# Loads of x, of its copy by tokens, of residuals and of factor sources tied behind the weights' loads in issue order, in an attention and pooling trunk

## The chip, the cores and the metric

The kernel runs on one core of a Trainium2 chip. Its time is the device time of one execution in microseconds (us), taken as the median of several runs. All transfers of this kernel are issued by one engine's queue, SyncE's (SP in the profile), and are carried by the core's 16 DMA engines.

## The reference

The program is a trunk of two layers over 4,096 tokens of width 1,024, all in float32, with a norm ahead of each layer, a residual after it and a norm at the end.

```python
for i in range(DEPTH):                       # DEPTH = 2
    h = rmsnorm(x, norm_g[i])
    y = attn_layer(h, ...) if i % 2 == 0 else pool_layer(h, ...)
    x = x + y
return rmsnorm(x, final_g)
```

The attention layer makes q (16 heads of 64), k and v (4 heads each) and a gate z with one projection, attends in a sliding window of 128 tokens with a learned sink per head, multiplies by silu(z) and projects back. The pool layer makes u and z, takes trailing means of u over 2, 4, 8 and 16 tokens, mixes them, gates and projects back.

## The kernel before

A float32 operand is split into a high and a low part, and each product is three passes of TensorE (`PASSES`, line 261). The attention layer goes over 8 groups of 512 tokens, called stages here, s = 0 to 7. A stage has up to 14 units of 48 matmuls of 128x512 each: `k`, `q0` to `q3`, `v`, `out0` to `out3` (the output projection of the group before) and `z0` to `z3`. A stage of s from 2 to 6 runs k, q0, v, out0, out1, q1, out2, q2, out3, z0, q3, z1, z2, z3; the units are numbered through, so that stage 2 has units 24 to 37, with v as unit 26, and the v units of stages 3 to 7 are 40, 54, 68, 82 and 96. The v unit is written the other way round, as 96 matmuls of 128x256 (line 280): `v_piece` goes over the four blocks of 128 tokens, and for each block first over the first four chunks of the width and then over the last four.

Between the matmuls of the units stand the 16 attention iterations of a stage, each in three steps: scores (`it_scores`, matmuls at line 385, then softmax on VectorE, ScalarE and GpSimd), the turn of the probabilities (`it_turn`, transposes at line 410, a cast at 417, differences at 418 and 425, selections on GpSimd) and the product with v (`it_pv`, matmuls at lines 440 and 441, additions at 448). Names such as `P1_3_2` or `m1_1_3_2` give stage, head group and block.

What moves through SP's queue, in the order of the queue:

- **Weights.** From the second stage on, a unit's split weights come back from memory in two halves of 1 MB (`w_again`, lines 159 to 162; `w26_0` and `w26_1` are the halves of unit 26). They rotate through three buffers, so a half can only be loaded when the half three places before it has been used up: `w26_1` takes the buffer of `w25_0`, which is free when q0 is halfway through.
- **x, transposed** (`xt_load`, line 177): four loads of 512 KB a stage, `xt3_0` to `xt3_3` for stage 3. They are scaled on VectorE by the norm's factors (`x_scale`, line 253) and split into h (`h_chunk`).
- **A copy of x by tokens** (`xm_load`, line 182): four loads of 512 KB that share the two buffers `xt` with the loads before. ScalarE squares and sums each (`xm_square`, line 189).
- **The norm's factors** (`spread`, lines 230 to 246): from the sums, VectorE (`ms`) and GpSimd (`rs`) make 1/root; SP writes it out (`rsq`, line 241) and, once that has landed, reads it back broadcast over the partitions (`bc`, line 245). `x_scale` waits for `bc`.
- **k's second copy** (`k_twice`, line 307): four small transfers `kt<-kt` that follow the casts of k on ScalarE (line 300) and the differences on VectorE (line 301).
- **Residuals** (`res_load`, line 458), 512 KB each, for the four `out` units, and the stores of their results.
- **Factor sources and factors for the pool layer** (`seven_load`, line 515, 512 KB; `seven`, lines 518 to 541): raw weights are loaded, split into parts on ScalarE, VectorE and GpSimd, and stored again (`w_u<-part_u` and the like, lines 524 and 541; in the lists of order `w7_...<-part7_...`).

The order of the work is made in two steps. Each piece is entered with a planned time, in units, by `at(t, fn, ...)`, and the pieces are sorted by it. All of the attention layer is then emitted inside a block with a scheduler (line 1103), which simulates the engines' time and reorders each engine's queue as it sees fit. A load that waits for nothing but a buffer may so be moved ahead of pieces that were planned earlier. The loads of the copy for the next stage were planned at unit 5.0 and after (`XM`, line 39), but stand in the queue at the start of the stage. The pool layer after the attention layer is emitted in the planned order.

Of the kernel before, what the change touches and what calls it, by code (L numbers as in the profile page):

```python
# [1 line left out]

# [33 lines left out]


STRIP = 56
XM = (4.0, 6.3)
SLOTS = dict(sr=1, sl=2)  # L40


# [5 lines left out]
def f32(ap):  # L48
    return ap.bitcast(F32)
# [3 lines left out]
def trunk_kernel(ctx, tc, xt, xm, ng, w_a_in, sinks, w_a_out, wu_t, wmix, pscale, w_b_z, w_b_out, fg, out):  # L53
    nc = tc.nc
# [21 lines left out]
    wparts = {}  # L76
# [62 lines left out]
    def at(t, fn, *args):  # L139
        events.append((t, len(events), fn, args))  # L140


    wtiles = {}
    wraws = {}

    def w_load(U, src, hf):
# [11 lines left out]

    def w_again(U, hf, key):
        t = lp.tile([128, 2, 4, UC], F32R, tag="w", bufs=3, name=f"w{U}_{hf}")  # L160
        nc.sync.dma_start(f32(t), wparts[key, hf])
        wtiles[U, hf] = t


# [5 lines left out]
    def xt_load(s, n):  # L170
        if s > 0:
            t = sp.tile([128, 2, G], F32, tag="xt", bufs=2, name=f"xt{s}_{n}")
        else:
            if n % 2 == 0:
                xts["pair"] = lp.tile([128, 2, 2, G], F32, tag=f"a{2 + n // 2}", name=f"xt{s}_{n}")
            t = xts["pair"][:, n % 2]
        nc.sync.dma_start(t, xt[s, n])
        xts[s, n] = t

    def xm_load(s, b):  # L180
        t = sp.tile([128, D], F32, tag="xt", bufs=2, name=f"xm{s}_{b}")
        nc.sync.dma_start(t, xm[s, b])
        xts[s, "m", b] = t

    def xm_square(s, b):
# [269 lines left out]

    def res_load(s, n):
        t = lp.tile([128, 2, G], F32, tag="res", bufs=2, name=f"res{s}_{n}")
        nc.sync.dma_start(t, xt[s, n])
        ress[s, n] = t

    def ev_o(U, s, n):
# [47 lines left out]
    def seven_load(key, src, hf):  # L509
        if hf == 0 and key[0] == "o":  # L510
            wout[key[1]] = [dram.tile([128, 2, 2, UC], F32, name=f"wo_{key[1]}_{i}") for i in range(4)]
        elif hf == 0:
            wseven[key] = [dram.tile([128, 2, 2, 2, 128], F32, name=f"w7_{key[0]}{key[1]}_{i}") for i in range(7)]
        t = lp.tile([128, 4, UC], F32, tag="wraw", bufs=2, name=f"raw7_{key[0]}{key[1]}_{hf}")
        nc.sync.dma_start(t, src[:, 4 * hf:4 * hf + 4, :])
        wraws[key, hf] = t

    def seven(key, hf):
# [324 lines left out]
    def unit(kind, s, j, t):  # L843
# [8 lines left out]
        if u == 0:  # L852
            for hf in range(2):
                at(-8.85, w_load, u, src, hf)
                at(-8.05, w_split, u, hf, key, nc.gpsimd if hf else nc.vector)
        elif s == 0:
            at(t - T["wl0"], w_load, u, src, 0)
            at(t - T["wl1"], w_load, u, src, 1)
            at(t - T["ws0"], w_split, u, 0, key, nc.gpsimd if kind in "qz" else None)
            at(t - T["ws1"], w_split, u, 1, key, None if kind == "out" else nc.gpsimd)  # L860
        else:
            at(t - T["wr0"], w_again, u, 0, key)
            at(t - T["wr1"], w_again, u, 1, key)
        if kind == "out":
            at(t - T["res"], res_load, s, j)
# [22 lines left out]
    for n in range(4):  # L888
        at(-9, xt_load, 0, n)
# [17 lines left out]
    for s in range(NG + 1):  # L907
# [16 lines left out]
        if s < NG:  # L924
# [7 lines left out]
            for i in range(16):  # L932
                j, b, t = i // 4, i % 4, base + sc[i]
# [3 lines left out]
            for j in range(4):  # L937
                t = max(base + order.index(("z", j)) + 1.0, base + sc[4 * j + 3] + turn + pv)
                at(t, gate_a, s, j)
        if s + 1 < NG:  # L940
            for n in range(4):
                at(base + XM[s > 0] + 0.9 * n - 1.3, xm_load, s + 1, n)
                at(base + XM[s > 0] + 0.9 * n, xm_square, s + 1, n)
                at(base + L + (-3.2, -3.0, -0.74, -0.49)[n], xt_load, s + 1, n)
            at(base + XM[s > 0] + 3.2, spread, s + 1)
            for k in range(NK):
                t = base + L - 1 + (k + 1) / 8 + T["hc"]
                t = base + L + 0.2 if k > 5 else t
                at(t if k > 3 else base + L - T["xs"] + k / 8, x_scale, s + 1, k)
                at(t, h_chunk, s + 1, k)  # L950
        if 2 <= s < NG:
            for i in range(4):
                k, hf = sevens[4 * (s - 2) + i]
                t = base + 2.0 + 3.2 * i
                at(t, seven_load, k, sources[k[0]][k[1]], hf)
                at(t + 0.8, seven, k, hf)
# [27 lines left out]
    for g in range(NP):  # L984
        ph = (g, "in")
        stream = [(ph, kind, j) for j in PAIRS for kind in "uz"]
        if g == 0:
            t0 = base - A_OUT
            at(t0 + 2.0, b_spread, ("h", 0))
            for i, p in enumerate(PAIRS):  # L990
                t = t0 + 6.0 * i
# [52 lines left out]
        for p in PAIRS:  # L1044
            for n in (0, 1):
                t = pos - (0, PROD, 5 * PROD, 7 * PROD)[p] + (0.1 if p > 1 else 0.3 if p else 0.5 + 5 * n)
# [3 lines left out]
        for x, j in enumerate(PAIRS):  # L1050
            u = (po, "o", j)
            at(op - 3.0 if x == 0 else pos - 8.0, o_open, u)
            if g == NP - 1 and x == 3:
                t = pos
# [99 lines left out]
```

## Time and profile before

| what | value |
|---|---|
| runs | 2660.74, 2655.14, 2654.10 us; median 2655.14 us |
| the profiled execution, its own time | 2661.88 us |
| its span, first to last instruction | 2660.1 us |
| TensorE (PE) busy | 2549.5 us, 96% of the span |
| VectorE (DVE), ScalarE (ACT), GpSimd (POOL) busy | 61%, 39%, 22% |
| mean granted TensorE clock | 0.983 of full speed |
| moved by DMA | 626 MB, SP's queue busy 69.7% of 16 engines' span |

The attention layer's stages 2 to 7 lie between 408 and 1613 us. In the profile PE is TensorE's matmul, PEld its weight load, SPq the issue of transfers from SP's queue. "idle before, releaser" is the time for which an engine did nothing ahead of an instruction, and what ended that. In rows of windows, each engine has its busy time with the number of its instructions, and the row ends with the granted clock of TensorE (1.00 is full speed), the mean busy share of the 16 DMA engines, and GB/s.

### The profile page before, as it was taken

Reading aid. Unit: us, or ns where it says so; the run is one execution under the profiler, and the core shown is the slowest. Engines: PE = TensorE matmul, PEld = TensorE weight load, DVE = VectorE, ACT = ScalarE, POOL = GpSimd, SP = SyncE. Lnnn points to the kernel's source line nnn. Section 1 sums busy time; section 2 is a strip of 40 time slices with the busy share of each in tenths; the row PEclk is TensorE's granted clock in tenths of the full one; section 3 lists DMA queues with packets and bytes.
Section 4 is the critical chain, followed back from the end, with each engine's and each line's share of the span. In section 5 each row is a group of like instructions: output and inputs, shape, how many; then the busy total and the mean of one; then the engine's idle time right before and its main releaser. Section 6 shows DMA issues by size and latency. Waiting matters only on the chain.

```text
span 2660.1 us, 35166 instructions
## 1 busy us (share of the span) xinstructions
PE 2549.5 (96%) x12604; PEld 2146.2 (81%) x12604; DVE 1612.3 (61%) x2537; ACT 1043.2 (39%) x2680; POOL 578.7 (22%) x883
## 2 busy tenths in 40 slices
PE   7999999999999999999998999999999999999997
PEld 5888888887887887887887887888878887887886
DVE  5377666566567567566566568648455665655544
ACT  4465545355345445444444443223312231332121
POOL 3554333233243242233332331000000000000000
PEclk8999999999999999999999999999999999999998
DMA  8865766677678677677677657667577668757752
GB/s 289 313 210 192 270 228 230 223 244 256 224 251 277 223 241 250 225 245 257 222 246 239 204 201 273 207 194 260 194 261 265 233 219 289 267 175 262 252 202 99
DMA packets 175193, 626.07 MB, mean 235 GB/s; under 512 B 23198, under 2 KB 33438, under 8 KB 145324
## 3 DMA queue, kind: packets, MB, share of 16 engines
q1 hardware_dynamic: 175020, 623.83, 69.7%
q8 instruction: 100, 1.64, 0.2%
q14 instruction: 73, 0.60, 0.1%
HBM read 489.47 MB, written 117.51 MB: 228 GB/s over the span
## 4 chain that ended last, share of the span: by engine, by line
PE 56%; DMA 16%; DVE 9%; ACT 2%; issue 2%; SPq 0%; POOL 0%; DVEq 0%; POOLq 0%; ACTq 0%
PE mm L270 19%; DMA fin<-x 3%; PE mm L280 3%; DMA w<-wparts 3%; DMA w_u<-part_u 2%; DMA out<-fin 2%; PE s L385 2%; DMA w_z<-part_z 2%; PE X_0u L628 2%; PE X_0z L628 2%; PE X_3z L628 1%; PE X_3u L628 1%; PE po L440 1%; PE X_2u L628 1%; PE pT L410 1%
## 5 line engine op out<-in xcount | busy, mean ns | idle before, releaser
L270 PE MATMUL mm<-h,w 128*128 128x512 f32 x3456 | 848.8, 396 | 9.1 <-DVE sz L354 4.5
L270 PEld LDWEIGHTS mm<-h,w 128*128 128x128 f32 x3456 | 638.5, 190 | 136.8 <-DVE sz L354 5.1
L270 PE MATMUL mm<-a,w 128*128 128x512 f32 x1536 | 372.2, 393 | 4.2 <-DMA w<-wparts 2.5
L270 PEld LDWEIGHTS mm<-a,w 128*128 128x128 f32 x1536 | 282.0, 188 | 61.2 <-issue 2.0
L426 POOL TENSOR_SCALAR_AFFINE_SELECT m<-m 64x256 fp32r<-64x256 f32 x256 | 117.7, 460 | 580.7 <-ACT m L417 572.3
L397 ACT ACTIVATE P<-s,mx 128x129 f32<-128x129 f32 x512 | 181.8, 370 | 34.8 <-DVE mx L394 32.4
L447 ACT COPY tmp<-po 64x256 f32<-64x256 f32 x256 | 94.1, 367 | 198.7 <-PE po L441 164.5
L755 POOL TENSOR_TENSOR rs<-ms,mhalf 128x4 f32<-128x4 f32 x7 | 7.0, 1007 | 735.8 <-DVE ms L754 735.8
L402 POOL TENSOR_TENSOR P<-P,sm 128x516 f32<-128x516 f32 x128 | 138.9, 1085 | 115.3 <-DVE sm L401 114.7
L448 DVE TENSOR_TENSOR o<-po,tmp 64x256 f32<-64x256 f32 x256 | 107.7, 421 | 84.0 <-ACT tmp L447 79.8
L385 PEld LDWEIGHTS s<-kt,q 128*128 128x128 f32 x1024 | 135.0, 193 | 8.7 <-ACT s L376 0.3
L427 POOL TENSOR_SCALAR_AFFINE_SELECT m<-m 64x256 fp32r<-64x256 f32 x256 | 120.2, 470 | 90.2 <-DVE m L425 81.5
L385 PE MATMUL s<-kt,q 128*128 128x192 f32 x1024 | 136.9, 273 | 0.0
L318 DVE SCALAR_TENSOR_TENSOR q<-mm,q 64x512 fp32r<-64x512 f32 x128 | 88.1, 688 | 77.4 <-ACT q L317 75.9
L280 PE MATMUL mm<-w,h 128*128 128x256 f32 x768 | 107.7, 302 | 25.1 <-DMA w<-wparts 25.1
L280 PEld LDWEIGHTS mm<-w,h 128*128 128x128 f32 x768 | 104.5, 210 | 26.9 <-DMA w<-wparts 26.4
L317 ACT ACTIVATE q<-mm 64x512 fp32r<-64x512 f32 x128 | 75.9, 593 | 104.3 <-DVE q L318 58.3
L425 DVE TENSOR_TENSOR m<-pT,m 64x256 fp32r<-64x256 f32 x256 | 108.1, 422 | 7.9
L397 ACT ACTIVATION_READ_ACCUMULATOR P<-s,mx 128x1 f32 x512 | 104.6, 204 | 0.0
L417 ACT CAST m<-pT 128x512 fp32r<-128x512 f32 x128 | 75.0, 586 | 70.7 <-PE pT L410 65.4
L390 DVE COPY_PREDICATED s<-mask,s 128x256 f32<-128x256 int8 x128 | 54.3, 424 | 78.8 <-PE s L385 59.4
L418 DVE TENSOR_TENSOR m<-pT,m 128x512 fp32r<-128x512 f32 x128 | 87.9, 687 | 14.6 <-ACT m L417 12.7
(359 smaller groups left out, 4478.9 us busy)
## 6 DMA issues: line engine op xcount, KB each, us to landing
w<-wparts SPq DMA_DIRECT2D x196, 1024.0 KB
wparts<-w SPq DMA_DIRECT2D x28, 1024.0 KB
xt<-in_xt SPq DMA_DIRECT2D x32, 512.0 KB
res<-in_xt SPq DMA_DIRECT2D x32, 512.0 KB
x<-res SPq DMA_DIRECT2D x32, 512.0 KB
xr<-x SPq DMA_DIRECT2D x32, 512.0 KB
xm<-in_xm SPq DMA_DIRECT2D x28, 512.0 KB
w_u<-part_u SPq DMA_DIRECT2D x56, 256.0 KB
```

The source lines that it names most:

```text
L270: nc.tensor.matmul(ps[:, c], w[:, wl, k % 4, 128 * c:128 * c + 128], rhs(k, hl), start=(k == 0 and i == 0), stop=(k == NK - 1 and i == 2))
L280: nc.tensor.matmul(ps[:, b], hts[s, k][:, hl, 128 * b:128 * b + 128], wtiles[U, k // 4][:, wl, k % 4], start=(k == 0 and i == 0), stop=(k ...
L318: nc.vector.scalar_tensor_tensor(dst[64 - r:128 - r], src, -SCALE, f32(dst[r:r + 64]), op0=ALU.mult, op1=ALU.subtract)
L385: nc.tensor.matmul(ps[:, 2 * c + u, 2 - 2 * u:194 - 2 * u], qs[s, j][:, c, 2 * b + u].rearrange("p r x -> p (r x)"), kt[:, j, hl, t:t + 19 ...
L397: nc.scalar.activation(P[:, i, 0:129], view(ps, 1 + 512 * (i // 2) + 319 * (i % 2), [(1, 129)]), AF.Exp, bias=mx[:, i:i + 1], scale=-1.0, ...
L402: nc.gpsimd.tensor_mul(P[:, :, 0:129], P[:, :, 0:129], sm.unsqueeze(2).to_broadcast([128, 4, 129]))
L425: nc.vector.tensor_sub(m2[other, u], pu[wr, u], f32(mu[wr, u, 0]))
L426: nc.gpsimd.affine_select(out=v[wr], in_=f32(mu[wr, u, 0]).rearrange("p c (r q) -> p c r q", r=2), **after)
L427: nc.gpsimd.affine_select(out=v[other], in_=f32(v[other]), **after)
L447: nc.scalar.copy(tmp[d:d + 64], pv[e:e + 64, r])
L448: nc.vector.tensor_add(dst, pv[d:d + 64, r], tmp[d:d + 64])
L628: nc.tensor.matmul(ps, w[:, p // 2, wl, p % 2], t[:, hl], start=(first and a == 0 and b == 0), stop=(a == 3 and b == 2), skip_group_check= ...
```

## The change

Every load of a weight half notes itself as the latest one (`queued["w"]`). The loads of x, of its copy by tokens, of the residuals and of the factor sources are then emitted under `behind_weights()`, which tells the scheduler to keep them behind that latest weight load in SP's queue. It is an edge of issue order only: no semaphore and no wait is added by it. Beside that, the second number of `XM` goes from 6.3 to 7.5: for the stages after the first, the loads of the copy are planned at units 6.2 to 8.9 (7.5 + 0.9 n - 1.3), its squares at 7.5 to 10.2 and the norm's factors at 10.7. Line numbers in the changed kernel are 6 to 10 higher around these functions.

```diff
--- before.py
+++ after.py
@@ -1,4 +1,4 @@
-from contextlib import ExitStack
+from contextlib import ExitStack, nullcontext
 
 import concourse.bass as bass
 import concourse.tile as tile
@@ -36,7 +36,7 @@
 
 
 STRIP = 56
-XM = (4.0, 6.3)
+XM = (4.0, 7.5)
 SLOTS = dict(sr=1, sl=2)
 
 
@@ -141,6 +141,12 @@
 
 
     wtiles = {}
+    queued = {}
+
+    def behind_weights():
+
+        return tc.issue_after(queued["w"].ins) if "w" in queued else nullcontext()
+
     wraws = {}
 
     def w_load(U, src, hf):
@@ -158,7 +164,7 @@
 
     def w_again(U, hf, key):
         t = lp.tile([128, 2, 4, UC], F32R, tag="w", bufs=3, name=f"w{U}_{hf}")
-        nc.sync.dma_start(f32(t), wparts[key, hf])
+        queued["w"] = nc.sync.dma_start(f32(t), wparts[key, hf])
         wtiles[U, hf] = t
 
 
@@ -174,12 +180,14 @@
             if n % 2 == 0:
                 xts["pair"] = lp.tile([128, 2, 2, G], F32, tag=f"a{2 + n // 2}", name=f"xt{s}_{n}")
             t = xts["pair"][:, n % 2]
-        nc.sync.dma_start(t, xt[s, n])
+        with behind_weights():
+            nc.sync.dma_start(t, xt[s, n])
         xts[s, n] = t
 
     def xm_load(s, b):
         t = sp.tile([128, D], F32, tag="xt", bufs=2, name=f"xm{s}_{b}")
-        nc.sync.dma_start(t, xm[s, b])
+        with behind_weights():
+            nc.sync.dma_start(t, xm[s, b])
         xts[s, "m", b] = t
 
     def xm_square(s, b):
@@ -455,7 +463,8 @@
 
     def res_load(s, n):
         t = lp.tile([128, 2, G], F32, tag="res", bufs=2, name=f"res{s}_{n}")
-        nc.sync.dma_start(t, xt[s, n])
+        with behind_weights():
+            nc.sync.dma_start(t, xt[s, n])
         ress[s, n] = t
 
     def ev_o(U, s, n):
@@ -512,7 +521,8 @@
         elif hf == 0:
             wseven[key] = [dram.tile([128, 2, 2, 2, 128], F32, name=f"w7_{key[0]}{key[1]}_{i}") for i in range(7)]
         t = lp.tile([128, 4, UC], F32, tag="wraw", bufs=2, name=f"raw7_{key[0]}{key[1]}_{hf}")
-        nc.sync.dma_start(t, src[:, 4 * hf:4 * hf + 4, :])
+        with behind_weights():
+            nc.sync.dma_start(t, src[:, 4 * hf:4 * hf + 4, :])
         wraws[key, hf] = t
 
     def seven(key, hf):
```

The first place is SP's queue at the start of stage 2, from unit 25's first half of weights to the second half of unit 26, which is v. Before:

```order
L161 DMA w25_0_3878<-wparts_1_0_366 128x2048
L182 DMA xm3_0_4519<-in_xm 128x1024
L182 DMA xm3_1_4615<-in_xm 128x1024
L182 DMA xm3_2_4758<-in_xm 128x1024
L161 DMA w25_1_3927<-wparts_1_1_446 128x2048
L182 DMA xm3_3_4877<-in_xm 128x1024
L177 DMA xt3_0_5330<-in_xt 128x1024
L161 DMA w26_0_4012<-wparts_2_0_508 128x2048
L177 DMA xt3_1_5392<-in_xt 128x1024
L241 DMA rsq_3_115<-rs_3_5177 128x4
L307 DMA kt_160<-kt_160 64x2x512 x2
L161 DMA w26_1_4052<-wparts_2_1_620 128x2048
```

And in the changed kernel:

```order
L167 DMA w25_0_3878<-wparts_1_0_366 128x2048
L167 DMA w25_1_3927<-wparts_1_1_446 128x2048
L167 DMA w26_0_4012<-wparts_2_0_508 128x2048
L467 DMA res1_0_4044<-in_xt 128x1024
L315 DMA kt_160<-kt_160 64x2x512
L167 DMA w26_1_4052<-wparts_2_1_620 128x2048
L315 DMA kt_160<-kt_160 64x2x512 x3
L167 DMA w27_0_4113<-wparts_14_0_2418 128x2048
```

Ahead of `w26_1` stood six loads of 512 KB for stage 3, the store of its norm's factors `rsq_3` and two transfers of k; now one residual and one transfer of k. The loads `xm3_0` to `xm3_3` now stand between the weights of units 31 to 34, and `rsq_3`, `xt3_0`, `bc3` and `xt3_1`, in this order, between `w35_1` and `w36_1`; `rsq_9`, factors for the pool layer, now stands ahead of `w35_1`. The v units of stages 3 to 7 have the same picture, with three transfers of k ahead of `w68_1` in stage 5. In stage 2, three stores of factors for the pool layer now stand ahead of `w27_1`.

The second place is ScalarE's queue at the same time, around the casts of k (`kt`) at the end of unit 24. Before:

```order
L189 ACTIVATE xm3_1_4615,mr_3_4728<-xm3_1_4615 128x1024
L376 COPY s1_3_3_3862<-nsink_146 128x2x2
L189 ACTIVATE xm3_2_4758,mr_3_4728<-xm3_2_4758 128x1024
L447 COPY tmp1_3_1_3936<-po1_3_1_3929 64x256
L300 CAST kt_160<-mm24_3871 64x512
L447 COPY tmp1_3_1_3936<-po1_3_1_3929 64x256
L189 ACTIVATE xm3_3_4877,mr_3_4728<-xm3_3_4877 128x1024
L417 CAST m1_1_3_2_3979<-pT1_3_2_3974 128x512
L300 CAST kt_160<-mm24_3871 64x512
L397 ACTIVATE P1_3_3_3959,sm1_3_3_3957<-s1_3_3_3862,mx1_3_3_3956 128x129 x4
L376 COPY s2_0_0_3964<-nsink_146 128x2x2
L300 CAST kt_160<-mm24_3871 64x512 x2
```

And in the changed kernel:

```order
L405 ACTIVATE P1_3_2_3857,sm1_3_2_3855<-s1_3_2_3754,mx1_3_2_3854 128x129 x4
L133 CAST h2_7_3906<-xt2_3_3801 128x512
L384 COPY s1_3_3_3862<-nsink_146 128x2x2
L455 COPY tmp1_3_1_3936<-po1_3_1_3929 64x256 x2
L405 ACTIVATE P1_3_3_3959,sm1_3_3_3957<-s1_3_3_3862,mx1_3_3_3956 128x129 x4
L425 CAST m1_1_3_2_3979<-pT1_3_2_3974 128x512
L384 COPY s2_0_0_3964<-nsink_146 128x2x2
L308 CAST kt_160<-mm24_3871 64x512 x4
```

The squares of the copy stood among the casts; now the four casts are in a row, and the squares `xm3_0` to `xm3_3` stand in units 30 to 34 of the stage, among the softmax and the casts of head groups 0 and 1. The same holds at the start of stage 1, where the squares of `xm2` stood.

The third place is VectorE's queue around the scaling of `xt3_0`, the first instruction there that needs `bc3`. Before, in the q0 and v units of stage 2:

```order
L448 TENSOR_TENSOR o1_3_3826<-po1_3_2_4026,tmp1_3_2_4033 64x2x128 x2
L418 TENSOR_TENSOR m1_1_3_3_4059<-pT1_3_3_4054,m1_1_3_3_4059 128x512
L425 TENSOR_TENSOR m2_1_3_3_4060<-pT1_3_3_4054,m1_1_3_3_4059 64x256 x2
L318 SCALAR_TENSOR_TENSOR q2_0_4091<-mm25_4005,q2_0_4091 64x8x64
L253 SCALAR_TENSOR_TENSOR xt3_0_5330<-xt3_0_5330,ng_sb_145,bc3_5181 128x512 x2
L253 SCALAR_TENSOR_TENSOR xt3_1_5392<-xt3_1_5392,ng_sb_145,bc3_5181 128x512 x2
L318 SCALAR_TENSOR_TENSOR q2_0_4091<-mm25_4005,q2_0_4091 64x8x64
L448 TENSOR_TENSOR o1_3_3826<-po1_3_3_4124,tmp1_3_3_4131 64x2x128
```

And in the changed kernel, in units 35 and 36:

```order
L398 COPY_PREDICATED s2_2_2_5247<-mask_154,s2_2_2_5247 128x2x2x64
L326 SCALAR_TENSOR_TENSOR q2_3_5374<-mm34_5217,q2_3_5374 64x8x64
L402 TENSOR_REDUCE mx2_2_2_5347<-s2_2_2_5247 128x4
L261 SCALAR_TENSOR_TENSOR xt3_0_5330<-xt3_0_5330,ng_sb_145,bc3_5309 128x512
L426 TENSOR_TENSOR m1_2_2_1_5364<-pT2_2_1_5359,m1_2_2_1_5364 128x512
L433 TENSOR_TENSOR m2_2_2_1_5365<-pT2_2_1_5359,m1_2_2_1_5364 64x256 x2
L261 SCALAR_TENSOR_TENSOR xt3_0_5330<-xt3_0_5330,ng_sb_145,bc3_5309 128x512
L456 TENSOR_TENSOR o2_2_5311<-po2_2_0_5312,tmp2_2_0_5319 64x2x128
L326 SCALAR_TENSOR_TENSOR q2_3_5374<-mm34_5217,q2_3_5374 64x8x64
```

The scaling stood among the evictions of q0 (`q2_0<-mm25`); now the first half of it stands ahead of the differences `m1` and `m2` of an attention iteration, and the scaling of `xt3_1` a few rows further, ahead of the last part of the eviction of q3 (`q2_3<-mm34`), whose buffer unit 36 needs.

## The prediction

> **What bounds the kernel now.** I read the busy times first, then what TensorE (PE) waits for, then the place of its largest wait on the timeline, in windows and in SP's queue. The change works in stages 2 to 7. One window holds them all, and beside it stand the waits of PE in it:
>
> ```profile
> 408.00:1613.00 1205.00, 1160.55 (x6122) 988.54 (x6121) 752.70 (x1335) 560.02 (x1670) 392.84 (x630) 0.98 0.71 236
> ```
>
> ```profile
> PE mm L280 <- DMA w<-wparts: 25.1, 6, 8.3
> PE po L441 <- POOL m L427: 4.9, 12, 0.6
> PE po L440 <- DVE o L448: 4.7, 6, 1.0
> PE pT L410 <- POOL P L402: 4.2, 8, 0.8
> ```
>
> PE is the bound: 1160.55 of 1205 us. It idles 44.45 us there, and 25.1 of them are one kind of wait: six times, once in each v unit, the matmuls of line 280 wait for weights. The rest are short waits in attention. On PE's timeline (start, duration) the wait looks as follows in stage 2 and in stage 7:
>
> ```profile
> 438.17 1.59 PE L280 MATMUL mm<-w,h 128*128 128x256 f32 x12
> ...
> 444.74 0.79 PE L280 MATMUL mm<-w,h 128*128 128x256 f32 x2 [4.87 <-DMA w<-wparts]
> ...
> 1447.43 2.93 PE L280 MATMUL mm<-w,h 128*128 128x256 f32 x12 [8.28 <-DMA w<-wparts]
> ```
>
> After 12 matmuls with the first half of the weights, v needs the second, 1.6 us after its start. SP's queue (start, duration, line) tells why it is late:
>
> ```profile
> 414.16 6.00 SPq L182 DMA_DIRECT2D xm<-in_xm  x3
> ...
> 423.22 0.33 SPq L182 DMA_DIRECT2D xm<-in_xm  x1
> 426.78 0.33 SPq L177 DMA_DIRECT2D xt<-in_xt  x1
> 427.16 0.43 SPq L161 DMA_DIRECT2D w<-wparts  x1
> 430.50 0.33 SPq L177 DMA_DIRECT2D xt<-in_xt  x1
> ...
> 433.95 1.89 SPq L307 DMA_DIRECT2D kt<-kt  x2
> 435.93 0.55 SPq L161 DMA_DIRECT2D w<-wparts  x1
> ```
>
> The second half is issued at 435.93, 2.2 us before v starts at 438.17. Its place in the queue is behind xt loads, which wait for a buffer of the copy by tokens, and behind two transfers of k. Those wait for k's casts on ScalarE, and these stand in turn behind the copy's squares. Stage 1 has none of this in the way of v's second half:
>
> ```profile
> 233.63 7.79 SPq L161 DMA_DIRECT2D w<-wparts  x2
> ```
>
> ```profile
> 240.91 1.72 PE L280 MATMUL mm<-w,h 128*128 128x256 f32 x13
> ```
>
> There it is issued 7.3 us ahead of v, and v doesn't wait. The DMA engines' share in these stretches (last three numbers: clock, DMA share, GB/s) tells how long the transfer takes:
>
> ```profile
> 234.40:238.20 3.80, 3.80 (x27) 3.37 (x26) 3.02 (x6) 2.45 (x8) 1.91 (x2) 1.00 0.79 276
> 238.20:241.80 3.60, 3.60 (x21) 3.09 (x20) 2.23 (x6) 2.11 (x8) 2.42 (x5) 1.00 0.02 5
> 435.93:444.74 8.81, 3.95 (x24) 3.32 (x22) 3.11 (x7) 2.14 (x4) 1.66 (x4) 0.97 0.98 237
> ```
>
> In stage 1 the engines are empty 4.6 us after the issue (233.63 to 238.20). In stage 2 they are full throughout, and the half takes 8.8 us (435.93 to 444.74).
>
> The wait costs more than its length, since a slower clock follows it:
>
> ```profile
> 444.74:447.58 2.84, 2.84 (x13) 2.84 (x14) 0.59 (x1) 0.09 (x1) 0.00 (x0) 0.50 1.02 372
> 447.58:456.75 9.17, 9.17 (x78) 9.17 (x78) 7.52 (x11) 2.88 (x5) 0.00 (x0) 1.00 0.15 30
> ```
>
> The granted clock is 0.50 for some 3 us, then 1.00, at which 78 matmuls take 9.17 us, 0.118 each. The six v units whole (PE alone: busy time with its count, clock, DMA share, GB/s):
>
> ```profile
> 438.17:456.75 18.58, 13.71 (x103) 0.91 0.57 159
> 637.39:656.38 18.99, 14.80 (x103) 0.82 0.63 168
> 837.58:858.54 20.96, 16.27 (x109) 0.84 0.72 222
> 1040.64:1058.90 18.26, 14.99 (x103) 0.81 0.67 178
> 1239.56:1256.86 17.30, 14.04 (x103) 0.90 0.77 176
> 1437.57:1459.93 22.36, 14.08 (x104) 0.85 0.69 188
> sum 116.45, PE 87.89; mean PE 14.65
> ```
>
> Their 625 instructions at 0.1176 us make 73.5 us, and PE was busy for 87.89: the slow clock costs 14.4 us. So the wait is worth 25.1 + 14.4 = 39.5 us at most.
>
> The Trainium skill, page "TensorE: Matmul & The Clock Gate", Part 1, has the rule that after an idle window of about 3.4 us the clock falls to half, and rises again after a busy one; the 4.87 us wait followed by 0.50 agrees. By its length alone, a wait cut below that window would cost no slow clock, and the rival of half the gain, below, would come out 7 us lower; but stage 4, the third row above (0.84), had only this wait for weights:
>
> ```profile
> 846.67 1.65 PE L280 MATMUL mm<-w,h 128*128 128x256 f32 x6 [1.27 <-DMA w<-wparts]
> ```
>
> **The change, part by part.** *The second half of v's weights.* Ahead of it in SP's queue now stand a residual and one transfer of k (three in stage 5). The first k transfer needs two of the four casts, which now follow each other:
>
> ```profile
> 425.60 1.06 ACT L189 ACTIVATE xm<-xm 128x1024 f32<-128x1024 f32 x1 [2.35 <-DMA xm<-in_xm]
> ...
> 429.32 1.06 ACT L189 ACTIVATE xm<-xm 128x1024 f32<-128x1024 f32 x1 [1.18 <-DMA xm<-in_xm]
> ...
> 434.67 0.58 ACT L300 CAST kt<-mm 64x512 fp32r<-64x512 f32 x1 [0.75 <-DVE kt L301]
> ```
>
> These two squares and their waits were 1.06 + 2.35 + 1.06 + 1.18 = 5.7 us of ScalarE's time ahead of the last cast, so that the casts end near 429.6 rather than 435.25. Then the buffer decides: the second half takes the buffer of q0's first half, free when q0 is half done. PE began q0 here:
>
> ```profile
> 425.90 6.19 PE L270 MATMUL mm<-h,w 128*128 128x512 f32 x26
> ```
>
> It had it until 438.17, so that the issue is due half of these 12.3 us, about 6.1, ahead of v. Bounds of the landing: 4.6 us after issue (stage 1's row) is 1.5 us ahead of v's start; 8.8 us (stage 2's) is 2.7 after it, 1.1 us too late. I take 6 us, nearer the quiet row, as the six loads of 512 KB that filled the engines have left; what remains there is one residual. That is 1.7 us early. Stage 7 loads no x for a next stage; there the load stood behind a store of factors for the pool layer, and these stores too have left the place, with their source, which is tied now:
>
> ```profile
> 1435.15 0.33 SPq L541 DMA_DIRECT2D w_z<-part_z  x1
> 1435.57 0.39 SPq L161 DMA_DIRECT2D w<-wparts  x1
> ```
>
> I leave 1 us for stage 5: the term is -24 us, and -13 of the 14.4 of slow clock.
>
> *The squares of the copy at stage 1's start.* PE waits there once:
>
> ```profile
> 222.62 0.77 PE L440 MATMUL po<-m,vm 128*128 128x256 f32 x2 [5.27 <-DVE m L425]
> ```
>
> The cast of that `m` stood on ScalarE behind squares; three of 1.06 us leave its way: -3.2 us (bounds 0 and -5.3).
>
> *The squares later.* 4 x 1.06 = 4.2 us of ScalarE a stage now stand in units 6 to 10, each behind its own load. ScalarE is busy 560 of 1205 us, and iterations of head groups 0 and 1 have room there; but a square that waits for its load (2.35 us above) holds back exps and casts queued behind it. Bounds: nothing, or all of 4.2 x 6 = 25 us; I take 0.5 us a stage, +3, since waits on ScalarE reach PE now only as the short rows 4.9, 4.7 and 4.2.
>
> *The norm's factors later.* `bc` now comes in units 35 and 36, with the scaling of xt ahead of an iteration's `m` on VectorE: while `bc` is away, VectorE stands, and behind it that iteration's differences, its selections on GpSimd, its product on PE, and the eviction of q3, whose buffer unit 36 needs. What the same wait is before:
>
> ```profile
> DVE xt L253 <- DMA bc<-rsq: 36.8, 6, 8.2
> ```
>
> It is 6.1 us each time, hidden under PE's wait for weights. That cover is gone. In its new place it stands about ten VectorE rows behind `ms`, so that most of the way of `rsq` and `bc` is used up by work. Bounds: 0, and 8.2 x 6 = 49 us on PE. I take 1 us on PE a stage, +6: PE has the matmuls of two units to go on with.
>
> *Residuals, xt and factor sources tied.* They are issued later, with buffers and users unchanged; xt is needed only for h, at the stage's end. Three factor stores ahead of `w27_1` and `rsq_9` ahead of `w35_1` are queued in front of weights; these are needed half a unit later at the earliest, so 0 (bounds 0 and, by one wait as long as v's mean of 4.2 us in each of six stages, +25). Their parts leave the k unit for places with more or less room: 0, with -5 (of the short waits) as the other end.
>
> Sum: -24 - 13 - 3.2 + 3 + 6 = -31.2 us. The profiled execution's own time was 2661.88 us (its span 2660.1 and 1.8 around it), so the same execution would take 2630.7. It lies 6.7 us above the median of the runs, 2655.14, and against that the forecast is 2624.
>
> **The rivals.** *Half the gain.* The half lands no sooner after its issue than before, since other loads fill the engines: 8.8 us as in stage 2, or 10.2 as the store of `rsq` in the rows below. Issued 6.1 us ahead and needed 1.6 after v's start, it is 1.1 to 2.5 us late, 1.8 x 6 = 11 us. Waits of that size may still bring half of the slow clock, 7 us. That takes 18 us off the 37 of the main term: 2642. For it speaks the DMA share of 0.98, against it that the six loads have left. Chance 0.16.
>
> *Another wait in its place.* PE's gain in v lets it reach attention's next steps sooner, and these are set by chains over four engines which ran on during the wait. Then the 37 us come back as waits for `m`, `o` and `P`: no change, about 2654. Against it speaks stage 1, whose v doesn't wait, with attention in between. Chance 0.10.
>
> *Slower, by the norm's factors.* `bc` follows a transfer out and a transfer back. If a full queue makes the way from `ms` to `bc` some 8 us longer than the VectorE rows between, PE loses 8.2 us a stage, 49 us, against gains of 40: with the +3 of the squares, 2655 + 12 = 2667. The turning point is (40 - 3) / 6 = 6.2 us of PE's time a stage. For it speaks how long the way takes behind full engines:
>
> ```profile
> 633.71 0.33 SPq L241 DMA_DIRECT2D rsq<-rs  x1
> ...
> 643.93 0.33 SPq L245 DMA_DIRECT2D bc<-rsq  x1
> ```
>
> The store needed 10.2 us there. Against it: that was in the same crowd of loads as v's weights. The Trainium skill, page "DMA: Bandwidth & Descriptors", Rules for kernel authors, speaks for this rival: issue early, compute, and wait late. By it, tying loads of x makes them cost, not gain; no run here has yet shown such a place late. Chance 0.07.
>
> That the change does nothing is excluded: the queue's order has changed at all six v units.
>
> **How the numbers follow.** The forecast has 0.67. A measurement of this kernel can tell about 0.3%, 8 us. Faster by more: forecast and half gain, 0.83; within: 0.10; slower: 0.07. The range's low end takes all of 39.5 + 5.3 and the short waits' 3: 2607. The high end lets the half gain in with all of the 6 us of `bc` doubled, 2650, and leaves out the last two cases, 0.17.
>
> **What would show it.** Right: in the profile after, line 280's wait for weights is gone or under 5 us in all; the second half is issued 6 us ahead of v; v units last 12 to 14 us at a clock of 1.00; waits for `bc` on VectorE show beside waits of PE for `m` near units 35 and 36 of 1 us or so. Wrong: line 280 still waits over 10 us (half gain); rows for `po` or `s` over 30 us (another wait); VectorE waits for `bc` as long as before and PE with it (slower).

## The result, and the profile after

The changed kernel's median is 2637.27 us (four runs, 2632.33 to 2638.89) against 2656.97 us before (four runs): a ratio of 0.9922, with a 95% interval of 0.9902 to 0.9942, or 19.7 us. The forecast was 2624 us, 13 us less; the rival of half the gain had 2642, 5 us more. The profiled execution took 2638.89 us, its span was 2637.1, which is 23.0 us under the span before.

The window of stages 2 to 7 is 21 us shorter. The waits of TensorE (PE) in it:

```profile
406.00:1590.00 1184.00, 1149.53 (x6122) 979.96 (x6120) 761.02 (x1347) 563.10 (x1683) 404.16 (x639) 0.99 0.73 245
```

```profile
PE po L449 <- DMA vq<-vq: 7.6, 5, 2.4
PE mm L288 <- DMA w<-wparts: 6.5, 2, 4.6
PE pT L418 <- POOL P L410: 4.7, 5, 1.4
PE po L448 <- DVE m L433: 4.6, 2, 3.0
PE mm L278 <- DMA w<-wparts: 3.5, 3, 2.4
```

The wait for v's weights (line 288 now) fell from 25.1 us to 6.5, and from six stages to two. A wait that wasn't there before stands at the top: `po` waits for a copy, `vq<-vq`. The out units wait for weights too (line 278). The six v units whole, as before (PE's busy time with its count, clock, DMA share, GB/s):

```profile
436.23:448.46 12.23, 12.23 (x103) 1.00 0.77 254
635.52:648.14 12.62, 12.49 (x104) 1.00 0.83 241
829.82:848.38 18.56, 13.98 (x104) 0.91 0.62 182
1029.48:1045.34 15.86, 13.98 (x103) 0.89 0.60 202
1225.64:1237.87 12.23, 12.23 (x104) 1.00 0.85 270
1418.41:1430.65 12.24, 12.24 (x104) 1.00 0.74 242
sum 83.74, PE 77.15; mean PE 12.86
```

Four of them now run through at the full clock in 12.2 to 12.6 us; stages 4 and 5 still stop. In SP's queue the second half of stage 2's weights is issued 6.35 us ahead of v's start at 436.23, with one transfer of k ahead of it:

```profile
429.14 0.63 SPq L315 DMA_DIRECT2D kt<-kt  x1
429.88 0.53 SPq L167 DMA_DIRECT2D w<-wparts  x1
430.50 3.03 SPq L315 DMA_DIRECT2D kt<-kt  x3
```

What was lost shows in three places. The first is v's end in stage 2. On ScalarE a cast of a factor part (`part_u`) waits for the store that frees its buffer, and v's own evictions stand behind it:

```profile
456.58 0.41 ACT L133 CAST part_u<-sum_u 128x256 fp32r<-128x256 f32 x1 [4.36 <-DMA w_u<-part_u]
456.89 1.00 ACT L343 CAST vp<-mm 64x1024 fp32r<-64x1024 f32 x1
...
459.51 1.01 ACT L343 CAST vq<-mm 64x1024 fp32r<-64x1024 f32 x1
```

In SP's queue the copies of `vp` and `vq`, and the weights between, follow the stores of these parts:

```profile
453.45 4.45 SPq L551 DMA_DIRECT2D w_u<-part_u  x2
458.00 0.38 SPq L167 DMA_DIRECT2D w<-wparts  x1
459.18 0.49 SPq L347 DMA_DIRECT2D vp<-vp  x1
461.81 0.48 SPq L348 DMA_DIRECT2D vq<-vq  x1
```

The copy of `vq` is issued 13.4 us after v's end at 448.46 (before, 9.8 us: 466.56 against 456.75), and PE waits for both copies in the first product with v:

```profile
471.49 0.36 PE L449 MATMUL po<-m,vp 128*128 128x256 f32 x1 [1.11 <-DMA vp<-vp]
...
473.95 0.36 PE L449 MATMUL po<-m,vq 128*128 128x256 f32 x1 [1.87 <-DMA vq<-vq]
```

The second place is the scaling of xt, which waits for `bc` on VectorE ahead of an iteration's `m`, and PE behind it:

```profile
571.25 0.75 DVE L261 SCALAR_TENSOR_TENSOR xt<-xt,ng_sb,bc 128x512 f32<-128x512 f32 x1 [5.62 <-DMA bc<-rsq]
```

```profile
573.65 0.47 PE L448 MATMUL po<-m,vm 128*128 128x256 f32 x2 [1.61 <-DVE m L433]
...
577.28 0.66 PE L418 MATMUL pT<-ident,P 128*128 128x128 f32 x4 [1.39 <-POOL P L410]
```

The third is v in stage 4, whose weights were issued as early as in stage 2 and landed far later, 12.45 us after their issue at 823.54:

```profile
835.99 2.31 PE L288 MATMUL mm<-w,h 128*128 128x256 f32 x11 [4.58 <-DMA w<-wparts]
```

The v units cut the span of every kernel into the same pieces; a unit counts from its first matmul to the first of the next unit. "v" is the sum of the six v units of stages 2 to 7, "between" is what lies between them, from the first one's start to the last one's end:

| piece, us | before | changed | difference |
|---|---|---|---|
| to v of stage 1 | 240.9 | 237.7 | -3.2 |
| from there to v of stage 2 | 197.3 | 198.5 | +1.2 |
| v | 116.5 | 83.7 | -32.7 |
| between | 905.3 | 910.7 | +5.4 |
| after the last v | 1200.2 | 1206.5 | +6.3 |
| span | 2660.1 | 2637.1 | -23.0 |

In the last piece two new waits of stage 7 are the like of those above, its out0 for weights and `po` for `vq`:

```profile
1452.51 2.57 PE L278 MATMUL mm<-a,w 128*128 128x512 f32 x10 [2.44 <-DMA w<-wparts]
...
1458.63 0.36 PE L449 MATMUL po<-m,vq 128*128 128x256 f32 x1 [1.61 <-DMA vq<-vq]
```

### The profile page after: what moved, and what is told of

Same layout as the page of the kernel before. It is cut to its first block, busy times and chain, and to the rows that moved or that the text cites. A ratio compares the mean times of both kernels' runs of the same rounds, so it can differ in the third digit from the quotient of the medians.

```text
span 2637.1 us, 35135 instructions
## 1 busy us (share of the span) xinstructions
PE 2537.4 (96%) x12604; PEld 2137.1 (81%) x12604; DVE 1612.7 (61%) x2537; ACT 1041.5 (39%) x2680; POOL 580.6 (22%) x883
## 4 chain that ended last, share of the span: by engine, by line
PE 35%; issue 30%; DMA 17%; DVE 12%; ACT 4%; POOL 2%; SPq 0%; POOLq 0%; DVEq 0%; ACTq 0%
PE mm L278 21%; PE s L393 2%; DMA vq<-vq 2%; DMA rsq<-rs 2%; DVE xt L261 1%; DMA w_u<-part_u 1%; PE mm L288 1%; PE pT L418 1%; DMA bc<-rsq 1%; PE po L448 1%; DMA wraw<-in_w_a_in 1%; DVE h L134 1%; DMA w_z<-part_z 1%; DMA raw_z<-in_w_b_z 1%; PE X_3z L638 1%
## 5 line engine op out<-in xcount | busy, mean ns | idle before, releaser
L326 DVE SCALAR_TENSOR_TENSOR q<-mm,q 64x512 fp32r<-64x512 f32 x128 | 88.1, 688 | 81.6 <-ACT q L325 79.8
L288 PE MATMUL mm<-w,h 128*128 128x256 f32 x768 | 99.2, 288 | 6.6 <-DMA w<-wparts 6.5
L288 PEld LDWEIGHTS mm<-w,h 128*128 128x128 f32 x768 | 96.9, 197 | 7.7 <-DMA w<-wparts 7.2
L402 DVE TENSOR_REDUCE mx<-s 128x4 f32<-128x516 f32 x128 | 88.7, 693 | 3.2
```

Source lines behind the costliest of these rows:

```text
L288: nc.tensor.matmul(ps[:, b], hts[s, k][:, hl, 128 * b:128 * b + 128], wtiles[U, k // 4][:, wl, k % 4], start=(k == 0 and i == 0), stop=(k ...
L326: nc.vector.scalar_tensor_tensor(dst[64 - r:128 - r], src, -SCALE, f32(dst[r:r + 64]), op0=ALU.mult, op1=ALU.subtract)
L402: nc.vector.tensor_reduce(mx.rearrange("p (c u) -> p c u", c=2), view(ps, 1, [(512, 2), (319, 2), (1, 129)]), axis=AX.X, op=ALU.min)
```

## The experiments

The theory with which I went in, called places: the change gains at v, since the second half of the weights is issued early, and loses in two places, at v's end by the factor parts among v's evictions, and in units 35 and 36 by the late `bc`. The rival, called traffic: what was lost was lost on the DMA engines, which the tied loads fill, whatever the order on the other engines. Each kernel was timed in five rounds beside the kernel before. Below, "ties" means `behind_weights()`, and the diffs are against the changed kernel if nothing else is said.

**The plan of the copy undone, all ties kept.**

```diff
-XM = (4.0, 7.5)
+XM = (4.0, 6.3)
```

> All four ties kept, the plan of the copy by tokens back at 6.3. Places (my theory: the change gains at v by the early second half, loses at v's end by the factor parts that stand among v's evictions on ScalarE and VectorE, and loses in units 35 and 36 by the late bc): the second half of v's weights stays as early as in the changed kernel, so line 280's wait stays at 0 to 7 us; bc lands long before the scaling, so VectorE's 38.7 us wait for bc falls under 10, and the waits of TensorE for m and P near units 35 and 36, about 9 us over stages 1 to 6, go with one slow clock: 6 to 11 us faster than the changed kernel, ratio to the kernel before 0.988 to 0.990. Traffic (the rival: what was lost, was lost since the tied loads fill the DMA engines beside the weights and v's copies, and the order on the other engines does not matter): no difference to the changed kernel, 0.992, and VectorE's wait for bc as before.

It took 2610.25 us, 0.9822 (0.9794 to 0.985): not 6 to 11 but some 27 us faster than the changed kernel. In the profile VectorE's wait for `bc` is gone from stages 1 to 6, as expected (the changed kernel's row, then this one's; one wait of 3.7 and 3.9 us in each lies in the first stage, at 55 us):

```profile
DVE xt L261 <- DMA bc<-rsq: 38.7, 7, 7.2
```

```profile
DVE xt L261 <- DMA bc<-rsq: 3.9, 1, 3.9
```

PE's waits for `po <- DVE m` and for `pT <- POOL P` from stage 1 on fell from 14.3 us to 2.6 (the rows of the two waits in either kernel). The waits at v's end, for `vq`, `vp` and out's weights, did not fall (16.8 us against 12.2), so they are no part of this gain. So the places theory has the sign, and its price was less than half of the real one; traffic, which expected no difference, falls here.

**The tie of the factor sources undone.**

```diff
     def seven_load(key, src, hf):
...
-        with behind_weights():
-            nc.sync.dma_start(t, src[:, 4 * hf:4 * hf + 4, :])
+        nc.sync.dma_start(t, src[:, 4 * hf:4 * hf + 4, :])
```

> The tie of the factor sources alone undone. Places: the parts leave v's end, so TensorE's waits for the vp and vq copies (8.7 us) fall under 2 and out0's waits for weights (3.5 us) go; in stages 4 and 7 stores of parts stand ahead of v's second half again, as in the kernel before, so line 280 waits 4 to 10 us there: near the changed kernel, 0.990 to 0.995. Traffic: the same stores and loads in other places, line 280's wait grows in stages 4 and 7 too, but waits for vp and vq stay above 5 us, as the copies are as big as before: 0.993 to 0.997.

It took 2635.91 us, 0.9917 (0.9893 to 0.9942), the changed kernel's time. The waits for `vq` and `vp` are gone altogether, and line 288 waits in all six v units instead:

```profile
PE mm L288 <- DMA w<-wparts: 12.0, 6, 5.3
```

v takes 93.4 us and what lies between 900.6: next to the changed kernel v loses 9.6 us and the rest gains 10.1. The time is as places expected, and the waits for `vq`, which traffic kept over 5 us, aren't there; but the wait of 4 to 10 us in stage 4 was 1.8, and the waits in stages 2, 3, 5 and 6 were not expected. Nor was this: with the plan still at 7.5, VectorE's wait for `bc` fell from 38.7 to 4.9 us. In stage 2 the scaling stands behind an iteration's `m` there, not ahead of it, and `bc` is issued at 561.05 rather than 566.35. So the late plan alone does not make that wait; the tie of the factor sources has a part in it.

**k's copies tied as well.**

```diff
     def k_twice():
         for r in (0, 1):
             v = f32(kt).rearrange("p (c r) l t -> p r c l t", r=2)[:, r]
             for l in range(2):
-                nc.sync.dma_start(v[64 - 64 * r:128 - 64 * r, :, l, 128:], v[64 * r:64 * r + 64, :, l, 128:])
+                with behind_weights():
+                    nc.sync.dma_start(v[64 - 64 * r:128 - 64 * r, :, l, 128:], v[64 * r:64 * r + 64, :, l, 128:])
```

> The changed kernel with k's copies tied as well, so that all four stand behind the second half of v's weights. Places: the second half goes out when its buffer is free, some 6 us ahead of v, with nothing of k ahead of it on the DMA engines; the waits left in stages 4 and 5 (6.5 us, and one slow clock of 1.7 us) fall under 2 us: 5 to 8 us faster than the changed kernel, 0.989 to 0.990. Traffic: the landing 12 us after the issue in stage 4 came from full engines, which stay full: the wait in stage 4 stays above 3 us, 0.991 to 0.993.

It took 2634.95 us, 0.9923 (0.9895 to 0.9952): no gain. v fell to 78.1 us, as expected, with stage 5's wait gone and 3.0 us left in stage 4. But between them it took 921.4 us, 10.7 more than the changed kernel; the waits for `vq` and for the out units' weights were 9.9 and 9.3 us. The time is the one that traffic expected, and the wait left in stage 4 lies at its bound of 3 us; the gain of 5 to 8 us that places expected didn't come. What made the rest longer is not shown.

**The factor sources planned 0.6 units later.**

```diff
-                t = base + 2.0 + 3.2 * i
+                t = base + 2.6 + 3.2 * i
                 at(t, seven_load, k, sources[k[0]][k[1]], hf)
                 at(t + 0.8, seven, k, hf)
```

> The changed kernel with the factor sources and parts planned 0.6 units later in each stage. Only two parts now stand ahead of v's last evictions and none that waits for a part's buffer. Places: ScalarE's wait of 4.36 us for a part's buffer ahead of the vp cast is gone, vq's copy is issued 10 us after v's end rather than 13, TensorE's waits for vp and vq fall from 8.7 to under 2 us and out0's for weights from 3.5 to under 1: 8 to 13 us faster than the changed kernel, 0.987 to 0.989. Traffic: the source's load and the stores of two parts are issued just ahead of the copies, so that the engines are as full when these are issued; waits for vp and vq stay above 5 us, 0.991 to 0.993.

It took 2620.3 us, 0.9863 (0.9834 to 0.9892), some 16 us under the changed kernel. From stage 1 on its waits for weights and for the copy of `vq` are:

```profile
PE mm L288 <- DMA w<-wparts: 2.5, 3, 2.0
...
PE po L449 <- DMA vq<-vq: 1.7, 3, 0.8
...
PE mm L278 <- DMA w<-wparts: 0.4, 1, 0.4
```

The part that waited for a buffer no longer stands ahead of v's evictions, and the waits for `vq` and for out's weights are gone, though the source and the first two stores are still issued just ahead of the copies. That settles the new wait at v's end for places, against traffic. VectorE still waits 25.8 us for `bc` here, so that the late `bc` is a loss of its own. But this wait fell too, from 38.7, and v from 83.7 to 78.8 us, so that the 16 us aren't all owed to v's end.

**Late factors or late squares.** The late plan moves two things, the copy's loads and squares, and the factors behind them. This kernel has the first as early as before and the second as late as the changed kernel:

```diff
-XM = (4.0, 7.5)
+XM = (4.0, 6.3)
...
-            at(base + XM[s > 0] + 3.2, spread, s + 1)
+            at(base + (10.7 if s > 0 else 7.2), spread, s + 1)
```

> All ties kept, loads and squares of the copy planned from 6.3 as in the run with the plan undone, but the norm's factors still planned at unit 10.7 as in the changed kernel: it parts the late bc from the late loads and squares. The run with the plan undone gave 0.982 against 0.992. Theory bc (the late factors cost those 25 us): VectorE waits for bc again, over 20 us in all, and the time is near the changed kernel, 0.989 to 0.993. Rival squares (the late loads of the copy and ScalarE's waits for them, 46 us in the changed kernel, cost them): near the run with the plan undone, 0.981 to 0.984, whatever VectorE waits for bc.

It took 2626.71 us, 0.989 (0.9876 to 0.9905): 18 of the 27 us come back with the late factors alone (the two intervals leave some 8 us of room either way), and VectorE waits for `bc` for 19.5 us in all, just under the 20 expected. That leaves some 9 us for the later squares; ScalarE's wait for the copy's loads is the same in the changed kernel and with the plan undone:

```profile
ACT xm L197 <- DMA xm<-in_xm: 46.0, 18, 4.8
```

```profile
ACT xm L197 <- DMA xm<-in_xm: 46.1, 22, 4.4
```

**The plan at 7.5 alone,** in the kernel before, without any tie.

```diff
-XM = (4.0, 6.3)
+XM = (4.0, 7.5)
```

> The kernel before with the plan of the copy at 7.5 alone, no tie. Theory (the ties are what moves the loads): the scheduler moves the loads of the copy to the stage's start as before, v's second half is as late as before, line 280 waits 20 to 28 us; the norm's factors move to units 35 and 36, and bc is waited for there: 0.998 to 1.008. Rival (the later plan takes the loads out of v's way by itself): line 280 waits under 10 us, 0.99.

It took 2671.79 us, 1.0061 (1.0047 to 1.0075), slower by 16 us. Line 286 (v) waits 21.7 us: by itself the plan moves no load out of v's way. What it adds is seen on VectorE in stage 2. The factors come late, and four scalings in a row stand ahead of `m`:

```profile
573.33 2.74 DVE L259 SCALAR_TENSOR_TENSOR xt<-xt,ng_sb,bc 128x512 f32<-128x512 f32 x4 [1.83 <-DMA bc<-rsq]
576.10 0.69 DVE L324 SCALAR_TENSOR_TENSOR q<-mm,q 64x512 fp32r<-64x512 f32 x1
576.83 0.69 DVE L424 TENSOR_TENSOR m<-pT,m 128x512 fp32r<-128x512 f32 x1
```

PE waits for `m` of that line for 11.3 us in eight places, where it was 1.5 us in the kernel before.

**The tie of the factor sources alone,** in the kernel before.

```diff
     def seven_load(key, src, hf):
...
-        nc.sync.dma_start(t, src[:, 4 * hf:4 * hf + 4, :])
+        with behind_weights():
+            nc.sync.dma_start(t, src[:, 4 * hf:4 * hf + 4, :])
```

> The kernel before with the tie of the factor sources alone. Theory places: xm and xt loads still stand ahead of v's second half in stages 2, 3, 5 and 6, so line 280 waits there 3 to 5 us each; stage 7, where stores of parts stood ahead, loses its 8.3 us wait; the parts come to v's end, and waits for vq and out0's weights of 5 to 10 us come in: 0.995 to 1.003. Rival (the factor sources are what filled the engines at v): line 280 waits under 8 us in all, 0.990 or less.

It took 2612.41 us, 0.9836 (0.9819 to 0.9853). Both expectations missed it: the time is the rival's, and line 286 still waits 14.1 us in five v units, which isn't. v fell from 116.5 to 94.2 us, what lies between from 905.3 to 886.3, and stage 1 from 197.3 to 192.3.

Most of v's 22.3 us are gained where stores of factor parts stood ahead of the second half: 10.1 in stage 7 and 7.7 in stage 4, as places expected of stage 7. These stores have left with their sources. In stage 7, where v starts at 1397.61, one transfer of k is left ahead of the half, and the wait of 8.28 us is gone:

```profile
1390.50 0.63 SPq L313 DMA_DIRECT2D kt<-kt  x1
1391.23 0.53 SPq L167 DMA_DIRECT2D w<-wparts  x1
```

In stages 3 and 6, with loads of x still ahead, the waits stay (4.18 and 5.33 us). Stage 2 gains 2.9 us with all the loads of x ahead. Why shows in SP's queue there, where v starts at 429.39:

```profile
418.30 0.38 SPq L167 DMA_DIRECT2D w<-wparts  x1
420.81 1.92 SPq L183 DMA_DIRECT2D xt<-in_xt  x2
422.93 0.33 SPq L167 DMA_DIRECT2D w<-wparts  x1
423.77 0.33 SPq L247 DMA_DIRECT2D rsq<-rs  x1
424.36 4.16 SPq L313 DMA_DIRECT2D kt<-kt  x4
```

The last of the xt loads goes out some 7 us ahead of v, as in the kernel before (430.50 against 438.17). What is different is the rows behind: the second half of the weights now stands ahead of `rsq` and k's transfers, and is issued 6.5 us ahead of v rather than 2.2. The tie changed nothing that belongs to this place; the scheduler, whose simulated times it shifted, put these the other way round.

What lies between gains in two ways. PE idles 7.5 us there rather than 15.9: its waits for `m`, `o` and `P`, 17.2 us in stages 2 to 7 before, are 2.5 here. And its busy time there is 878.8 us rather than 889.4, for the same work. Which of the moved parts does this is not shown.

**The plan undone and the factor sources later, with all ties.**

```diff
-XM = (4.0, 7.5)
+XM = (4.0, 6.3)
...
-                t = base + 2.0 + 3.2 * i
+                t = base + 2.6 + 3.2 * i
```

> A version from the runs so far: all ties, the plan of the copy at 6.3, and the factor sources 0.6 units later. If the two losses of the changed kernel (late bc, parts at v's end) are apart, their gains add: 0.982 (plan undone) less some 0.006 (parts later): 0.975 to 0.979, with waits for vq, for out0's weights and for bc all under 5 us. If the two share a cause, it stays at 0.980 to 0.983.

It took 2599.56 us, 0.9789 (0.9775 to 0.9802): the upper end of what adding the two gains gave, some 35 us under the changed kernel by the ratios. From stage 1 on, only v's weights are waited for more than 3 us:

```profile
PE mm L288 <- DMA w<-wparts: 7.1, 4, 2.7
PE mm L278 <- DMA w<-wparts: 2.5, 2, 2.1
```

**The ties of x, its copy and the residuals alone, plan at 6.3.** The edit is that of the run without the factor tie, and the plan undone.

> Ties of x, its copy and the residuals alone, plan at 6.3. So far against the kernel before: factor tie alone 0.984, all ties 0.982, all ties but the factors' and plan 7.5 0.992, plan 7.5 alone 1.006. Theory plan (the plan at 7.5 costs 16 to 27 us wherever it is put, and both kinds of tie take the same wait away at v, so that one of them does most): without the plan this comes out 16 to 25 us under the run without the factor tie, 0.982 to 0.986. Rival factor (the factor tie is what gains, the ties of x add little): 0.990 to 0.997, with line 280 waiting over 12 us.

It took 2624.89 us, 0.9883 (0.986 to 0.9906), between the two expectations: the plan costs 9 us here, not 16 to 25.

**The tie of the factor sources alone, plan at 7.5.** The edit is that of the run with the factor tie alone, and the plan at 7.5.

> The factor tie alone with the plan at 7.5: the loads of the copy go to the stage's start again, and only the norm's factors come late, to units 35 and 36. Theory plan: slower than the factor tie alone by 12 to 25 us, 0.988 to 0.993, with waits of VectorE for bc or of TensorE for m at units 34 to 36. Rival (the plan costs only together with the ties of x): within 6 us of the factor tie alone, 0.982 to 0.986.

It took 2638.7 us, 0.9938 (0.9917 to 0.9958): the plan costs 27 us here. VectorE waits for `bc` for 39.6 us, and PE from stage 1 on for `P` and `m`:

```profile
PE pT L416 <- POOL P L408: 9.1, 9, 2.0
...
PE po L446 <- DVE m L431: 6.7, 2, 4.3
```

**The best so far with k's copies tied.** The edit is that of the run with all ties, the plan undone and the sources later, and that of k's copies above.

> The best so far (all ties, plan 6.3, factor sources 0.6 units later, 0.979) with k's copies tied behind v's second half: its three waits at v, 7.1 us in all with two slow clocks, fall under 4 us if the copies ahead of the half made them late: 0.976 to 0.978. If the half lands late for full engines whatever is ahead: 0.978 to 0.981.

It took 2599.54 us, 0.9788 (0.9763 to 0.9814): the same time. v is down to 74.7 us with a wait of 1.0 us left, so k's copies did make the half late; but stage 1 grew from 193.0 to 199.0, where out waits 4.7 us for `vq`'s eviction on VectorE, and what lies after the last v from 1202.5 to 1207.0.

**The best so far without the ties of x.** The kernel before with the factor tie and the sources 0.6 units later.

> The best so far without the ties of x, its copy and the residuals: the factor tie alone, with the factor sources 0.6 units later. If the ties of x are worth what line 280 still waits without them (14.1 us and some slow clock in the run with the factor tie alone), it is 8 to 18 us slower than the best, 0.982 to 0.986. If they are worth nothing next to the factor tie: 0.977 to 0.981.

It took 2615.57 us, 0.9847 (0.9821 to 0.9873), 16 us slower than with the ties of x: these are worth that much next to the factor tie, mostly between the v units (894.2 us against 881.6). And by itself the later source gains nothing here. One row of this run bears on the late factors:

```profile
DVE xt L259 <- DMA bc<-rsq: 30.7, 6, 8.1
```

26.8 us of it lie in the v units of stages 2 to 6, where the scaling stands with the plan at 6.3. From stage 1 on PE waits only 0.3 us for `m` and 0.6 for `P`. So the length of VectorE's wait is not its price: that depends on what stands behind it and how soon PE needs it.

The runs together, as ratios to the kernel before, and the two pieces of the profiled executions:

| kernel | plan 6.3 | v, between | plan 7.5 | v, between |
|---|---|---|---|---|
| no tie | 1 | 116.5, 905.3 | 1.0061 | 108.2, 922.3 |
| x, copy, residuals tied | 0.9883 | 88.1, 898.4 | 0.9917 | 93.4, 900.6 |
| factor sources tied | 0.9836 | 94.2, 886.3 | 0.9938 | 88.9, 903.6 |
| all tied | 0.9822 | 77.5, 897.4 | 0.9922 | 83.7, 910.7 |
| all tied, sources later | 0.9789 | 84.8, 881.6 | 0.9863 | 78.8, 898.1 |

Where the factor sources are tied and planned as before, the plan at 7.5 costs 27 us, with and without the ties of x, and VectorE waits for `bc` for 35 us after the first stage. Where they aren't tied, it costs 16 us, or 9 with the ties of x, and these waits are 6 and 2 us.

## Why the prediction came out, and where it was off

The time lies nearer to the rival of half the gain than to the forecast, but that rival's mechanism, a half that lands no sooner after its issue, came true only in stages 4 and 5 (12.45 and 8.8 us). Of the signs named, the wait for v's weights was 6.5 us, between the 5 that would show the forecast right and the 10 that would show it wrong, and four of the six v units ran at a clock of 1.00. The sign of the slower rival came as well: VectorE waited for `bc` as long as before (38.7 us against 36.8), and PE was held up by a part of it.

*v's second half.* The forecast took 24 + 13 = 37 us off v; the changed kernel's v units lost 32.7. The issue 6.1 us ahead of v was 6.35, and a landing in time was right for four stages of six. Stages 4 and 5 still waited, 6.5 us where 1 us was left. Why stage 4's half landed so late is open in part: with k's copies tied behind it the wait fell from 4.58 to 3.0 us in the changed kernel and from 2.19 to 1.0 in the fastest, so that these copies have a share.

But the reason given first, that the loads of x stood ahead of the weights, is one of three. The factor tie alone took 22.3 us from v, the ties of x alone 28.4, and both 39.0: they overlap by 11.7 us. Of the 22.3, 17.8 came in stages 4 and 7, where stores of factor parts stood ahead; the forecast had these stores for stage 7. In stage 2 it was the order against k's transfers, named in the forecast in second place.

The forecast also held a row of stage 4, a wait of 1.27 us and then a clock of 0.84, against the rule on idle windows. PE had stood for 0.37, 1.91, 0.59 and 0.55 us more in that unit, waiting for attention, 4.7 of 9.1 us in all, so that this row says little on short waits. Better ones are at the end.

*The start.* -3.2 us to v of stage 1, as forecast, but by luck. The wait itself only fell from 5.27 to 3.78 us; it is for an iteration's `P` now. And with the factor tie alone, where the squares stand in the way as before and the wait is 5.01 us, the same piece is 3.8 us shorter too.

*The later plan.* The forecast priced the late squares at 3 us and the late factors at 6. With all ties the plan costs 27 us (0.9922 against 0.9822), some two thirds of it by the factors. The mechanism was the one described, VectorE standing for `bc` ahead of `m`, and its length was near that of the row quoted then (five waits of 6.6 us on average in v, the sixth in the first stage; 5.6 us in the row above). The place hid it there, not PE's wait for weights: in the last run above the same wait costs PE next to nothing, though v waits for weights for 6.0 us in all. What failed is the discount to 1 us a stage on the ground that "PE has the matmuls of two units to go on with": in the rows above a late `m` stops PE for 1.61 us at the next `po`, though matmuls of a unit follow in its queue, and then for 1.39 us for the next iteration's `P`, 3.0 us in that stage where the forecast had 1. A slower clock comes on top: for the same work between the v units PE was busy for 889.2 us with the late factors alone, and for 881.0 with the plan undone.

*Factor sources tied: the step that failed.* Apart from stage 7's half of v, it stood at 0, with -5 as the gain at most. By itself the tie gains 44 us (0.9836), and beside the ties of x at plan 6.3 it gains 16 (0.9822 against 0.9883). At plan 7.5 it is worth nothing beside them (0.9922 against 0.9917), so that the sum wasn't hurt, but not since it does nothing: v gains 9.6 us and what lies between loses 10.1. With it come PE's waits for `vq` and `vp`, 8.7 us, and for out's weights, 3.5 us, of which the forecast had neither, and most of VectorE's wait for `bc`. Only the stores ahead of `w27_1` were looked at there, not the casts on ScalarE that wait for those stores.

So the time came out near by errors that offset each other: all ties at plan 6.3 are worth 47 us, where the forecast's terms for them make 40, and the plan costs 27, where they make 9. The slower rival had the right place: 18 us by the late factors lie between the 6 of the forecast and the 49 of that rival. And of the rival of another wait in v's place, a part came true at v's end.

## What to carry to other kernels

An edge that ties one load shifts a scheduler's simulated times everywhere: read the new order at each place that waits, and test each tie alone, since their gains may not add: 44 us and 31 us alone made 47 together. A load taken out of the way has a consumer: follow it to the engine where the consumer stands, and price a stall there by what stands behind it in that engine's order: next to nothing where the bound engine needs that late, several us a stage where it needs it next. Of moved work, look at what it waits for itself: a cast that waits for the store of its buffer holds up every eviction queued behind it.

## What the runs showed of the hardware

A half of 1 MB took 4.6 us from issue to the engines' rest in stage 1 before, and 12.45 us in stage 4 after, with the engines busy all the while:

```profile
823.54:835.99 12.45, 7.87 (x46) 6.61 (x44) 5.14 (x9) 3.62 (x7) 1.66 (x4) 1.00 0.98 246
```

In stage 2 the same load with the same rows ahead of it landed within 7.9 us, as v didn't wait 1.6 us after its start.

Waits of TensorE of about 2 us were sometimes followed by a slower clock and sometimes not: stage 5 of the changed kernel had one of 1.88 us and a clock of 0.89 over its v unit, and the run with the factor tie alone two, 1.35 us in stage 2 and 2.39 in stage 5, with 1.00. The row of the latter:

```profile
1009.55:1024.42 14.87, 12.48 (x104) 1.00 0.71 218
```

The Trainium skill, page "TensorE: Matmul & The Clock Gate", Part 1, has a window of about 3.4 us that runs free of the program; it would explain the chance in it, but not that 1.88 us were enough, since TensorE was not idle for a window of that length.

One kernel's runs lay up to 20 us apart (2602.02 to 2621.88 with all ties and plan 6.3, where the profile is that of the slowest), so that a profile's pieces and the medians can differ by some 10 us.
